# Three more places for the raw output weights of layer 0's feed-forward, and another scratch tile for layer 1's squares

## The chip, the cores and the metric

One core of one Trainium2 chip runs the whole kernel in one launch. The metric is the device time of one execution in microseconds (us); shown is the median of several runs. The engines are TensorE (PE in the profile), VectorE (DVE), ScalarE (ACT), GpSimd (POOL) and SyncE (SP), which issues nearly all transfers.

## The reference

Two layers over 512 latent tokens (x) and 256 context tokens (ctx), model width 1024. Each layer is a mixer (attention) followed by a SwiGLU feed-forward, both behind an RMS norm that is scaled, shifted and gated by a modulation worked out from the conditioning. Cut to what the change touches:

```
x   = x   + gx2 * swiglu(rms(x,   norm_ffn_w) * (1 + scx2) + shx2, ffn_w_in, ffn_w_out)   # layer 0, 512 tokens
ctx = ctx + gc2 * swiglu(rms(ctx, norm_ffn_w) * (1 + scc2) + shc2, ffn_w_in, ffn_w_out)   # layer 0, 256 tokens
swiglu(h) = (silu(gate) * up) @ w_out,   gate, up = split(h @ w_in)                       # hidden width 2816
hx  = rms(x, norm_mix_w) * (1 + scx1) + shx1                                              # start of layer 1
rms(x, w) = x * rsqrt(mean(x*x) + 1e-6) * w
```

## The kernel before

Tokens are handled in six tiles of 128: t = 0 to 3 are latent, 4 and 5 context. The hidden width 2816 is handled in 22 F-tiles of 128 (f = 0 to 21). Every fp32 operand of a matrix product is split in two: a high part (a cast on ScalarE) and a low part (raw minus high, a subtraction mostly on VectorE); each product is then three matmuls, high x high, high x low, low x high. `split_into` (lines 1023 to 1026) does this for both operands of the output product.

`way_out0` (from line 1028) is the second half of layer 0's feed-forward, hidden times `ffn_w_out`. Its 12 sums (6 token tiles x 2 halves of the width) don't fit the PSUM banks at once, so it makes two passes over the F-tiles: pass 0 (p = 0) for t = 4, 5, 0 and pass 1 for t = 1, 2, 3, six sums each. For each F-tile `ready_hid` loads the hidden tile from DRAM (tile `raw`, line 1041) and the weight tile of 128x1024 (tile `wr`, named wdr in the profile, line 1043) and splits both; then `sums` does 6 x 3 matmuls (lines 1057 to 1059). The last two F-tiles are held back (`held = 2`) and are summed bank by bank, so that the residual of one bank (`residual`, lines 480 and 481) runs under the next bank's matmuls. Four of the six banks of pass 1 are banks that pass 0 has used; pass 1 can write them when their residuals are done.

Places in SBUF:

- Raw weights come from a ring of two places, tag "raw" (`raw_tile`, line 90), which also serves other loads of the kernel. A place is free again when the low part of its tile is done.
- Split weights of pass 0 go into four fixed places (`places`, parts of the tile hT), so F-tile f waits until TensorE has finished f-4. Raw hidden tiles have two places (`raws`).
- Pass 1 splits into tiles of the pool of this stage (`out0`), with tags "wdh" and "wdl" for the weights, three places each. Pass 0 doesn't use these.

A hook in the loop advances the modulation of layer 1 (`mod_stream`), which loads 512 KB tiles (modw, line 211) in the same time and works on them on ScalarE, VectorE and GpSimd; other hooks finish norms and load early weights of layer 1.

Behind `way_out0` layer 1 begins. `factor` (line 329) squares a token tile on ScalarE with the sum as a second output and works out the norm's factor on GpSimd. The squares themselves are not wanted; they are written to a scratch tile, `spare`, for t = 1, 2 and 3. `last_norm0(t)` (line 1630) takes two tiles, h and hc: h is x times the factor (line 345, GpSimd, in `norm_steps`), which TensorE transposes (line 352); hc takes the transposes scaled and shifted (lines 358 and 360), which are then split into hT. The tiles come from the ring "xo" of six places that also holds the token tiles, but for t = 1 one of the two is `spare`. TensorE's order there is: sums of t = 4, norm of t = 1, sums of t = 5, norm of t = 2, half the sums of t = 0, norm of t = 3.

TensorE's instructions keep the order in which the program is written (a manual schedule). Those of the other engines, SyncE's transfers among them, are ordered by a planner that runs the program against modelled times: of what is ready, the earlier in the program goes first. Each engine then works through its own queue in order.

Of the kernel before, what the change touches and what calls it, by code (L numbers as in the profile page):

```python
# [11 lines left out]
F32 = mybir.dt.float32  # L12
# [7 lines left out]
P = 128  # L20
D = 1024
KT = D // P
# [41 lines left out]
def backbone(es: ExitStack, tc: tile.TileContext, x, c, ctx, c_ctx, mod_w, mod_b, norm_mix_w, norm_ffn_w,  # L64
# [25 lines left out]
    def raw_tile(shape, name):  # L90
        return keep.tile(shape, F32, name=name, tag="raw", bufs=2)
# [208 lines left out]
    def gate_row(l, part, i, pool):  # L300

        if (l, part, i) not in gmem:
            gate_mem(l, part, 1)
        g = pool.tile([P, D], F32, name=f"g{i}", tag=f"g{i}")
        with tc.issue_after(turn["load"].ins):
            nc.sync.dma_start(g.rearrange("p (k c) -> p k c", c=P), dram_rows(gmem[l, part, i]))
        return g
# [26 lines left out]
    def norm_steps(t, xt, l, f, pool, tags=(("nh", 2), ("nhc", 2)), room=None, bank=tr_tile, to=None, pool_scale=False, r=None):  # L334

        i = 0 if t < NTX else 1
        h, hc = room or (pool.tile([P, KT, P], F32, name=name, tag=tag, bufs=n)
                         for name, (tag, n) in zip(("nh", "nhc"), tags))  # L340
        halves = hc if isinstance(hc, list) else [hc[:, 0:4], hc[:, 4:8]]
        xt = xt.rearrange("p (k c) -> p k c", c=P)
        r = factor(xt, h) if r is None else r
        if pool_scale:
            turn["pool_scale"] = nc.gpsimd.tensor_scalar(h, xt, r, 1.0, ALU.mult, ALU.mult)
        else:
            turn[f"scaled{t}"] = nc.scalar.activation(h, xt, AF.Copy, scale=r)
        yield
        for g in range(2):
            pt = bank("npt", [P, 4, P])  # L350
            for k in range(4):
                turn["npt"] = nc.tensor.transpose(pt[:, k, :], h[:, 4 * g + k, :], ident)  # L352
            ks = slice(4 * g, 4 * g + 4)
            for k in range(4):
                kk = 4 * g + k
                sc, sh = aff[l][:, f, kk, i:i + 1], modc[l][:, 3 * f, kk, i:i + 1]
                if g:
                    nc.scalar.activation(halves[g][:, k], pt[:, k, :], AF.Identity, bias=sh, scale=sc)
                else:
                    nc.vector.tensor_scalar(halves[g][:, k], pt[:, k, :], sc, sh, ALU.mult, ALU.add)  # L360
            hi, lo = (to(j, g) if to else tile_T(j, t)[:, ks] for j in range(2))
            turn["hi"] = nc.scalar.copy(hi, halves[g])
            (nc.gpsimd if g and not pool_scale else nc.vector).tensor_sub(lo, halves[g], f32(hi))
# [113 lines left out]
    def residual(xt, ps, g, n, pool=None, eng=nc.vector, rb=2):  # L477

        tmp = ps if pool is None else pool.tile([P, 512], F32, name="rtmp", tag="rtmp", bufs=rb)
        nc.vector.tensor_mul(tmp, ps, g[:, n * 512:(n + 1) * 512])  # L480
        eng.tensor_add(xt[:, n * 512:(n + 1) * 512], xt[:, n * 512:(n + 1) * 512], tmp)
# [541 lines left out]
    def split_into(to, src):  # L1023
        hi, lo = to
        nc.scalar.copy(hi, src)
        nc.vector.tensor_sub(lo, src, f32(hi))

    def way_out0(xs, hidm, pool, places, raws, hook, hooks, done):

        held = 2  # L1030
        g = [gate_row(0, 5, i, pool) for i in range(2)]
        for p, tiles in enumerate(((4, 5, 0), (1, 2, 3))):
            banks = [p_1.tile([P, 512], F32, name="dps", tag=tag) for tag in (("tr0", "tr1"), ("acc0", "acc1"))[p]]
            banks += [singles.pool.tile([P, 512], F32, name="dps", tag=tag, bufs=2) for tag in ("p1", "p1", "p0", "p0")]
            sums_of = [(t, n) for t in tiles for n in range(2)]
            ready = {}

            def ready_hid(f):
                raw = pool.tile([P, 3, P], F32, name="hr", tag="hr", bufs=3) if p else raws[f % len(raws)]
                for a, b, t in ((0, 2, 4), (2, 3, 0)) if not p else ((0, 3, 1),):  # L1040
                    nc.sync.dma_start(raw[:, a:b], hidm[f][:, t * P:(t + b - a) * P].rearrange("p (t c) -> p t c", c=P))
                wr = raw_tile([P, D], "wdr")
                turn["load"] = nc.sync.dma_start(wr, ffn_w_out[0, f * P:(f + 1) * P, :])
                if p:
                    w = [pool.tile([P, 4, 256], F32R, name=name, tag=name, bufs=3) for name in ("wdh", "wdl")]
                    h = [pool.tile([P, 3, P], F32R, name=name, tag=name, bufs=3) for name in ("hdh", "hdl")]
                else:
                    w, h = places[f % len(places)]
                split_into(w, wr.rearrange("p (k c) -> p k c", k=4))
                split_into(h, raw)  # L1050
                ready[f] = h, w

            def sums(f, i):
                (t, n), ps = sums_of[i], banks[i]
                hh, hl = (z[:, tiles.index(t)] for z in ready[f][0])
                a, b = (z[:, 2 * n:2 * n + 2, :] for z in ready[f][1])
                nc.tensor.matmul(ps, hh, a, start=f == 0, stop=False)
                nc.tensor.matmul(ps, hh, b, start=False, stop=False)
                nc.tensor.matmul(ps, hl, a, start=False, stop=f == NF - 1)

            for f in range(NF - held):
                ready_hid(f)
                for i in range(len(sums_of)):
                    sums(f, i)
                hook(p, f)
                for call in hooks.get((p, f), ()):
                    call()
            for f in range(NF - held, NF):
                ready_hid(f)
            for i, (t, n) in enumerate(sums_of):  # L1070
                for f in range(NF - held, NF):
                    sums(f, i)
                residual(xs[t], banks[i], g[0 if t < NTX else 1], n)
                done(t, n)
# [115 lines left out]
    for t in CTX_FIRST:  # L1190
        h = start.pool.tile([P, D], F32, name="nh", tag="nh", bufs=2)
# [125 lines left out]
    if True:  # L1317
# [93 lines left out]
        i = len(steps) - 1  # L1411
# [216 lines left out]
            late.pop(0)[1]()  # L1628

    def last_norm0(t):  # L1630
        h, hc = (spare if t == 1 and not i else raw_tile([P, KT, P], "nhc") if t == 2 and i else
                 keep.tile([P, KT, P], F32, name="nh", tag="xo", bufs=6) for i in range(2))
        with tc.high_priority(300):
            for _ in norm_steps(t, xs[t], 1, 0, None, room=(h, hc), pool_scale=True, r=factors.get(t)):
                pass

    if True:
# [8 lines left out]
        spare = keep.tile([P, KT, P], F32, name="nh", tag="xo", bufs=6)  # L1646
# [6 lines left out]
        for t in CTX_FIRST[:2]:  # L1653
            first.sums(t, banks[t], range(KT))
            ready(t)
            last_norm0(t - 3)
        first.sums(0, banks[0], range(4))
        last_norm0(3)
        first.sums(0, banks[0], range(4, KT))
        ready(0)  # L1660
# [311 lines left out]
```

## Time and profile before

| | us |
|---|---|
| median of 3 runs (lowest to highest) | 1685.1 (1684.14 to 1687.23) |
| profiled execution | 1686.72 |
| its span | 1684.9 |
| TensorE busy in it | 1629.0 (97%) |
| VectorE busy | 1145.2 (68%) |
| ScalarE busy | 934.8 (55%) |
| GpSimd busy | 713.2 (42%) |

The granted TensorE clock was 0.994 of full speed over the span. Rows of a timeline read: start, duration, engine, line, operation, output <- input, shape, count, and in brackets how long the engine had been idle before and what ended the idle time. Rows of windows read: stretch, its length, then busy time and count of TensorE, its weight loads, VectorE, ScalarE and GpSimd, then granted clock, busy share of the 16 DMA engines, GB/s. Rows of waits read: engine and line, what it waited for, total us, times, longest. All times in rows are us from the span's start.

### The profile page before, as it was taken

Reading aid. Unit: us, or ns where it says so; the run is one execution under the profiler, and the core shown is the slowest. Engines: PE = TensorE matmul, PEld = TensorE weight load, DVE = VectorE, ACT = ScalarE, POOL = GpSimd, SP = SyncE. Lnnn points to the kernel's source line nnn. Section 1 sums busy time; section 2 is a strip of 40 time slices with the busy share of each in tenths; the row PEclk is TensorE's granted clock in tenths of the full one; section 3 lists DMA queues with packets and bytes.
Section 4 is the critical chain, followed back from the end, with each engine's and each line's share of the span. In section 5 each row is a group of like instructions: output and inputs, shape, how many; then the busy total and the mean of one; then the engine's idle time right before and its main releaser. Section 6 shows DMA issues by size and latency. Waiting matters only on the chain. (4 is left out here: it accounts for less than half of the span.)

```text
span 1684.9 us, 28521 instructions
## 1 busy us (share of the span) xinstructions
PE 1629.0 (97%) x10376; PEld 1467.9 (87%) x10376; DVE 1145.2 (68%) x1980; ACT 934.8 (55%) x2008; POOL 713.2 (42%) x872
## 2 busy tenths in 40 slices
PE   6999999899999999999999999999999999999998
PEld 3977787677999999998878799999988899999887
DVE  3765756554799987767767666666666598887433
ACT  5466665745455655544564456666666555555320
POOL 2665555621345554412413367766765332221000
PEclk8999999999999999999999999999999999999999
DMA  9221321421455555439965221111113333331431
GB/s 321 70 71 52 93 70 51 163 63 38 120 178 173 166 159 164 135 110 334 305 185 192 91 58 44 48 42 47 45 51 100 113 96 110 104 105 53 138 100 63
DMA packets 221692, 194.67 MB, mean 116 GB/s; under 512 B 20016, under 2 KB 206960, under 8 KB 221552
## 3 DMA queue, kind: packets, MB, share of 16 engines
q1 hardware_dynamic: 221200, 192.65, 36.9%
q8 instruction: 81, 1.33, 0.3%
q14 instruction: 59, 0.48, 0.1%
q10 hardware_dynamic: 352, 0.21, 0.0%
HBM read 179.94 MB, written 12.87 MB: 114 GB/s over the span
## 5 line engine op out<-in xcount | busy, mean ns | idle before, releaser
L928 ACT CAST wbh<-wr 128x512 fp32r<-128x512 f32 x170 | 104.8, 621 | 122.9 <-PE p L960 67.7
L960 PE MATMUL p<-hT,wbh 128*128 128x256 f32 (+1 forms) x752 | 154.1, 298 | 0.0
L474 PE MATMUL inps<-wih,hT 128*128 128x384 f32 x512 | 143.9, 343 | 2.4 <-ACT qkv L688 1.7
L938 POOL TENSOR_TENSOR wbl<-wr,wbh 128x512 fp32r<-128x512 f32 x43 | 58.9, 1369 | 174.2 <-ACT wbh L928 174.2
L960 PEld LDWEIGHTS p<-hT,wbh 128*128 128x128 f32 x752 | 122.1, 191 | 0.2
L938 DVE TENSOR_TENSOR wbl<-wr,wbh 128x512 fp32r<-128x512 f32 x127 | 107.8, 860 | 19.8 <-ACT wbh L928 15.8
L960 PE MATMUL p<-hT,wbl 128*128 128x256 f32 (+1 forms) x376 | 111.8, 297 | 0.0
L960 PE MATMUL p<-t,wbh 128*128 128x384 f32 (+1 forms) x480 | 110.9, 317 | 0.0
L231 POOL TENSOR_TENSOR modp<-modp 128x512 f32<-128x512 f32 x40 | 57.5, 1437 | 111.8 <-ACT modp L230 111.8
L613 POOL TENSOR_SCALAR Pt<-Pt,rc 128x256 f32<-128x256 f32 (+3 forms) x96 | 75.3, 796 | 66.1 <-DVE rc L610 58.5
L960 PE MATMUL p<-hTt,wbh 128*128 128x256 f32 (+1 forms) x480 | 100.9, 302 | 0.0
L914 POOL TENSOR_TENSOR wr<-wr 128x512 f32<-128x512 f32 x40 | 62.2, 1556 | 91.1 <-DVE ws L919 88.8
L474 PEld LDWEIGHTS inps<-wih,hT 128*128 128x128 f32 x512 | 93.4, 188 | 5.4 <-ACT qkv L688 2.8
L960 PE MATMUL p<-b,wbh 128*128 128x384 f32 x368 | 93.5, 335 | 0.6 <-DVE c L988 0.6
L928 ACT CAST wbh<-ws 128x512 fp32r<-128x512 f32 x120 | 69.5, 580 | 43.7 <-PE p L960 28.5
L224 DVE SCALAR_TENSOR_TENSOR ma<-modw,cols,ma 128x256 f32<-128x256 f32 x140 | 91.5, 654 | 2.3
L601 ACT ACTIVATE Pt<-sc,nm 128x256 f32<-128x256 f32 (+3 forms) x96 | 67.7, 708 | 34.0 <-DVE nm L597 16.0
L474 PE MATMUL inps<-wil,hT 128*128 128x384 f32 x256 | 85.8, 335 | 0.0
L938 DVE TENSOR_TENSOR wbl<-ws,wbh 128x512 fp32r<-128x512 f32 x120 | 81.7, 681 | 1.7 <-ACT wbh L928 1.6
L960 PEld LDWEIGHTS p<-t,wbh 128*128 128x128 f32 x480 | 82.8, 189 | 0.0
L960 PEld LDWEIGHTS p<-hTt,wbh 128*128 128x128 f32 x480 | 78.4, 191 | 3.0 <-ACT modp L230 2.1
L474 PE MATMUL inps<-wihi,hT 128*128 128x384 f32 x256 | 76.6, 356 | 2.1 <-DVE modc L279 1.9
(357 smaller groups left out, 5219.1 us busy)
## 6 DMA issues: line engine op xcount, KB each, us to landing
modw<-in_mod_w_dram SPq DMA_DIRECT2D x96, 512.0 KB, 4.8
wr<-in_ffn_w_in_dram SPq DMA_DIRECT2D x176, 256.0 KB, 3.0
wdr<-in_ffn_w_out_dram SPq DMA_DIRECT2D x66, 512.0 KB, 3.6
wir<-in_od_w_in_dram SPq DMA_DIRECT2D x96, 128.0 KB, 2.3
hidm<-hid SPq DMA_DIRECT2D x44, 192.0 KB, 1.9
hr<-hidm SPq DMA_DIRECT2D x22, 192.0 KB, 3.5
x<-in_x_dram SPq DMA_DIRECT2D x8, 512.0 KB, 3.6
wir<-in_ev_w_in_dram SPq DMA_DIRECT2D x16, 256.0 KB, 3.4
```

Source lines behind the costliest of these rows:

```text
L224: nc.vector.scalar_tensor_tensor(acc, w[:, k], scale[k], acc, ALU.mult, ALU.add)
L231: nc.gpsimd.tensor_add(pr[:, 0:2], pr[:, 0:2], pr[:, 2:4])
L474: nc.tensor.matmul(ps, hs[j][:, k, :], ws[k // 2][z][:, k % 2, c0:c1], start=(k, j, z) == (0, 0, 0), stop=(k, j, z) == (KT - 1, 1, 0))
L601: turn["exp"] = nc.scalar.activation(p[:, :n], s, AF.Exp, bias=nm[:, c1], accum_out=sm[:, c1])
L613: nc.gpsimd.tensor_scalar(p[:, :n], p[:, :n], rc[:, hh:hh + 1], 1.0, ALU.mult, ALU.mult)
L914: nc.gpsimd.tensor_sub(w, raw[f, "G1"], w)
L928: nc.scalar.copy(hi, w)
L938: (nc.gpsimd if name == "G2" else nc.vector).tensor_sub(lo, raw[need[n]], f32(hi))
L960: nc.tensor.matmul(ps, w[:, k, :], H[b][h][:, k, :], start=first and k == 0 and q == 0, stop=final and k == 3 and q == 2, skip_group_check ...
```

## The change

In `ready_hid`, pass 0 takes the raw weight tile of f = 0 to 8 from the ring "raw" as before; from f = 9 on it takes it from the pool of the stage, with the tag "wdl" and three places, the ring in which pass 1 later puts its low parts (same size). Pass 1's raw weights come from the ring "raw" as before. In `last_norm0`, `spare` for t = 1 is now hc and no longer h; h is a tile of the ring "xo". The squares still write `spare`, which is thus a different tile from h.

```
                 for a, b, t in ((0, 2, 4), (2, 3, 0)) if not p else ((0, 3, 1),):
                     nc.sync.dma_start(raw[:, a:b], hidm[f][:, t * P:(t + b - a) * P].rearrange("p (t c) -> p t c", c=P))
-                wr = raw_tile([P, D], "wdr")
+                wr = (raw_tile([P, D], "wdr") if p or f < 9 else
+                      pool.tile([P, D], F32, name="wdr", tag="wdl", bufs=3))
                 turn["load"] = nc.sync.dma_start(wr, ffn_w_out[0, f * P:(f + 1) * P, :])
...
     def last_norm0(t):
-        h, hc = (spare if t == 1 and not i else raw_tile([P, KT, P], "nhc") if t == 2 and i else
+        h, hc = (spare if t == 1 and i else raw_tile([P, KT, P], "nhc") if t == 2 and i else
                  keep.tile([P, KT, P], F32, name="nh", tag="xo", bufs=6) for i in range(2))
```

More of the change, by code (lines that the diff above doesn't have):

```diff
@@ L1041, in ready_hid @@
                     nc.sync.dma_start(raw[:, a:b], hidm[f][:, t * P:(t + b - a) * P].rearrange("p (t c) -> p t c", c=P))
-                wr = raw_tile([P, D], "wdr")
+                wr = (raw_tile([P, D], "wdr") if p or f < 9 else
+                      pool.tile([P, D], F32, name="wdr", tag="wdl", bufs=3))
                 turn["load"] = nc.sync.dma_start(wr, ffn_w_out[0, f * P:(f + 1) * P, :])
@@ L1630, in last_norm0 @@
     def last_norm0(t):
-        h, hc = (spare if t == 1 and not i else raw_tile([P, KT, P], "nhc") if t == 2 and i else
+        h, hc = (spare if t == 1 and i else raw_tile([P, KT, P], "nhc") if t == 2 and i else
                  keep.tile([P, KT, P], F32, name="nh", tag="xo", bufs=6) for i in range(2))
```

## The prediction, as recorded before the result was known

> **What bounds the kernel now.** I read the page first, then busy time by stretch around the changed code, then what TensorE waited for there, and last the rows of each engine in time.
>
> ```profile
> PE 1629.0 (97%) x10376; PEld 1467.9 (87%) x10376; DVE 1145.2 (68%) x1980; ACT 934.8 (55%) x2008; POOL 713.2 (42%) x872
> ```
>
> ```profile
> 840.00:850.00 10.00, 7.60 (x33) 5.74 (x32) 6.50 (x8) 6.03 (x10) 3.12 (x2) 1.00 0.73 228
> 850.00:860.00 10.00, 8.64 (x36) 6.20 (x35) 7.75 (x11) 6.04 (x9) 1.48 (x4) 1.00 0.66 213
> ```
>
> ```profile
> PE dps L1057 <- DVE x L481: 1.4, 3, 0.9
> PE npt L352 <- POOL nh L345: 1.3, 1, 1.3
> PE dps L1057 <- ACT hT L1025: 1.3, 1, 1.3
> PE dps L1058 <- DVE hT L1026: 1.1, 1, 1.1
> PE inps L474 <- DVE hT L363: 0.6, 1, 0.6
> ```
>
> TensorE is busy for 97% of the span of 1684.9 us, so only its gaps can be won: 56 us in all. In the two passes of way_out0 (about 759 to 951 us) it has gaps in one place, around 840 to 860 us, where pass 0 ends and pass 1 begins: 2.40 + 1.36 us by the second fence. The third fence (TensorE's waits from 720 to 1000 us) names the causes: two waits on the split of pass 0's last weights (L1025 on ScalarE, L1026 on VectorE), three on residual additions of pass 0 (L481), and, after way_out0, one on the scaling of layer 1's norm (L345 on GpSimd). The first two causes belong to the first edit, the last to the second.
>
> What a gap costs is more than the wait, since the matmuls after it also come slower. So I count matmuls. The rows are TensorE's, in time.
>
> ```profile
> 833.84 0.39 PE L1057 MATMUL dps<-hT,hTt 128*128 128x512 f32 x1
> ...
> 842.00 0.39 PE L1057 MATMUL dps<-hT,hTt 128*128 128x512 f32 x1
> ...
> 853.13 0.39 PE L1057 MATMUL dps<-wdh,hdh 128*128 128x512 f32 x1
> ...
> 858.75 0.40 PE L1057 MATMUL dps<-wdh,hdh 128*128 128x512 f32 x1
> ```
>
> From 833.84 to 842.00 stand 36 undisturbed matmuls: 8.16 us, 0.2267 each, so an F-tile of 18 takes 4.08. The 36 of the last two F-tiles, 842.00 to 853.13, take 11.13: 2.97 lost. The first 15 of pass 1, 853.13 to 858.75, take 5.62 instead of 3.40: 2.22 lost. Together 5.19 us.
>
> **First edit: places for raw weights.** The rows are SyncE's, ScalarE's and VectorE's.
>
> ```profile
> 833.25 0.46 SPq L1043 DMA_DIRECT2D wdr<-in_ffn_w_out_dram  x1
> ...
> 835.75 6.37 SPq L1043 DMA_DIRECT2D wdr<-in_ffn_w_out_dram  x2
> ```
>
> ```profile
> 839.45 1.05 ACT L1025 CAST hT<-wdr 128x1024 fp32r<-128x1024 f32 x1 [4.01 <-DMA wdr<-in_ffn_w_out_dram]
> ...
> 843.10 1.03 ACT L1025 CAST hT<-wdr 128x1024 fp32r<-128x1024 f32 x1
> ```
>
> ```profile
> 834.49 1.23 DVE L1026 TENSOR_TENSOR hT<-wdr,hT 128x1024 fp32r<-128x1024 f32 x1 [1.19 <-ACT hT L1025]
> ```
>
> ```profile
> SPq L1043 <- DVE hT L1026: 22.7, 18, 2.4
> ```
>
> The raw ring has two places, and 18 of the weight loads wait for the low split that frees one (last fence, SyncE's waits from 745 to 862 us). The row at 834.49 splits f=19 and ends at 835.72; f=21's load is issued at 835.75 into that place. f=20's, issued at 833.25, can be cast only at 839.45. So a place is held for about 6.2 us of transfer and 2.3 of cast and low split, 8.5 in all; two places give one tile per 4.25 us, while TensorE takes one per 4.08. The reserve wears off, and f=21's cast at 843.10 comes after TensorE's f=20 products for the first bank.
>
> From f=9 on the change gives three places of its own. Three of 8.5 us give a tile per 2.8 us, so the transfer no longer sets the pace; the four places of split weights do, which keep a tile ready up to four ahead (16.3 us). f=21 can then be split when TensorE is done with f=17, about 12 us before it is needed. The first loss, 2.97, goes. ScalarE and VectorE do the same casts and low splits as before, only earlier; no instruction is added, and the DMA count and bytes stay.
>
> The second loss is one step further on. The rows are ScalarE's and VectorE's.
>
> ```profile
> 852.00 1.05 ACT L1025 CAST wdh<-wdr 128x1024 fp32r<-128x1024 f32 x1 [1.53 <-DMA wdr<-in_ffn_w_out_dram]
> ```
>
> ```profile
> 851.64 0.69 DVE L480 TENSOR_TENSOR dps<-dps,g 128x512 f32<-128x512 f32 x1
> 853.08 1.23 DVE L1026 TENSOR_TENSOR wdl<-wdr,wdh 128x1024 fp32r<-128x1024 f32 x1 [0.74 <-ACT wdh L1025]
> 854.22 0.69 DVE L480 TENSOR_TENSOR dps<-dps,g 128x512 f32<-128x512 f32 x1
> 854.82 0.68 DVE L481 TENSOR_TENSOR x<-x,dps 128x512 f32<-128x512 f32 x1
> ```
>
> Between the multiply (851.64) and the add (854.82) that free a bank, VectorE stands idle for pass 1's third weight tile, cast at 852.00 when its transfer lands. In the changed kernel the two raw places are free from the splits of f=7 and f=8 on (about 790 us), so pass 1's first two tiles load some 50 us earlier. Their low halves need places of the ring that now holds pass 0's raw weights; these come free with the splits of f=19 to f=21, before the residuals. Residual pairs then run behind TensorE: the third bank's products end three pairs of F-tile sums (3 x 1.36 = 4.1 us) before pass 0's end, pass 1 wants that bank 1.36 us after it, and a pair of multiply and add takes 1.3 us. Even three low splits of 1.23 between them fit the 5.4 us. I take the whole 2.22.
>
> What could eat it: f=9, 10 and 11 need no earlier tile, so SyncE can issue them early, when the first loads of pass 0 are still under way.
>
> ```profile
> 780.00:800.00 20.00, 20.00 (x90) 16.58 (x89) 14.97 (x21) 11.07 (x20) 9.00 (x8) 1.00 1.02 345
> ```
>
> ```profile
> 768.00:770.00 2.00, 2.00 (x11) 1.65 (x10) 1.82 (x4) 0.73 (x1) 0.00 (x0) 1.00 1.10 348
> ...
> 825.00:830.00 5.00, 5.00 (x24) 4.14 (x23) 4.86 (x7) 3.83 (x8) 1.98 (x2) 1.00 0.87 273
> 830.00:835.00 5.00, 5.00 (x24) 4.14 (x23) 3.81 (x6) 3.22 (x7) 2.66 (x4) 1.00 0.74 221
> ```
>
> ```profile
> 763.19 0.51 ACT L1025 CAST hTt<-hTt 128x384 fp32r<-128x384 f32 x1 [4.99 <-PE dps L1058]
> ...
> 784.28 1.06 ACT L1025 CAST hT<-wdr 128x1024 fp32r<-128x1024 f32 x1 [0.79 <-DMA wdr<-in_ffn_w_out_dram]
> ```
>
> ```profile
> L1057 PE MATMUL dps<-hT,hTt x132: 387/389/502, 759.0 to 852.5; 128*128 128x512 f32 x132
> ```
>
> At 768 us the DMA engines move 348 GB/s at a share over 1, so three loads of 512 KB ahead of the others cost these at most 4.5 us. f=8 is cast at 784.28 and split by 788; TensorE starts at 759.0 and wants f=8 after 8 x 4.08 us, at 791.6. A delay of 4.5 would miss that by 0.9 us; I take 0, since some of that delay falls into time in which the splits wait for TensorE anyway (763.19, f=4, 4.99 us), and keep 0 to 4.5 us for the range. It cannot go below nothing: TensorE is busy for all of 780 to 800, so nothing is to be won there.
>
> [...]
>
> **Second edit: the square's scratch.** The rows are TensorE's and GpSimd's, then the readers of x.
>
> ```profile
> 953.89 0.28 PE L474 MATMUL inps<-wil,hTc 128*128 128x256 f32 x1
> 954.01 0.28 PE L474 MATMUL inps<-wih,hTc 128*128 128x256 f32 x1
> 955.64 1.09 PE L352 MATMUL npt<-cst,nh 128*128 128x128 f32 x8 [1.34 <-POOL nh L345]
> ```
>
> ```profile
> 948.88 0.55 POOL L160 TENSOR_TENSOR rs_n<-rs_n,neghalf 128x1 f32<-128x1 f32 x1
> ...
> 954.47 1.12 POOL L345 TENSOR_SCALAR nh<-x,rs_n 128x1024 f32<-128x1024 f32 x1 [2.25 <-ACT nh L331]
> ...
> 957.10 1.12 POOL L345 TENSOR_SCALAR nh<-x,rs_n 128x1024 f32<-128x1024 f32 x1
> ```
>
> ```profile
> L347 ACT ACTIVATE nh<-x,rs_n x3: 1151/1152/1160, 855.0 to 876.0; 128x1024 f32<-128x1024 f32 x3
> ```
>
> The squares of t=1, 2 and 3 all write the tile spare, and before the change h of t=1 is that tile. Its factor is ready at 949.43 (948.88 + 0.55), yet the scaling starts at 954.47, after the last square. After the change h of t=1 is another tile of the ring and only hc, written after the transposes, is spare. The tiles of x that way_out0 is done with (t=4, 5, 0) were read last by 877.2, so three places are free: spare, h of t=1, h of t=2. The scaling can run at about 949.5 and end by 950.7, and the transposes follow the sums at once. The gap from 954.01 to 955.64 less the usual 0.12 is 1.51 us. Next on that path is h of t=2, used after 3.2 us of sums and 0.8 of transposes, 958.1 in the old count; it ended at 958.22 with GpSimd late and comes some 5 us sooner now. hc's wait for the last square is over before its first write. Bounds: 0 to 1.51; I take 1.51, and 0.5 us back for TensorE meeting the later wait on L363 (0.6 us in the third fence) sooner.
>
> **Sum.** 2.97 + 2.22 + 1.51 - 0.5 = 6.2 us. The profiled execution took 1686.72, 1.6 above the median of 1685.1; it would take 1680.5, and the median 1678.9, say 1679.
>
> **Rivals.** First, transfers are the bound: then places only change the order of waiting, the first edit gives nothing and the second 1.5: 1683.6. For it speaks the share over 1 until 825 us, against it the unfilled 825 to 835. Second, the early loads delay f=6 to f=8, TensorE wants these before the reserve has grown, and the whole bound of 4.5 us opens as a gap before f=9: 1683.4. Third, slower: pass 1's first two low halves are ready when their raw tiles land (about 800 us), and if they take two of the three places then, f=12 to f=21 go through one, held for 8.5 us. That is 4.4 us a tile over TensorE's pace: ten tiles cost 44 us, less the 16.3 of reserve, 28 in place of the 2.97; with the other gains about 1706. It decides from the sixth or seventh such tile on. Against it: pass 0's loads stand first in program order and have been waiting for a place all along. Fourth, the second edit only swaps its wait for one on another engine: 1680.4. Fifth, the queues of all engines but TensorE are ordered anew behind the change, and layer 1's attention gives back what was won:
>
> ```profile
> 1240.00:1260.00 20.00, 17.68 (x109) 15.98 (x108) 13.35 (x27) 12.58 (x32) 13.42 (x24) 0.92 0.16 53
> 1260.00:1280.00 20.00, 17.36 (x117) 14.74 (x115) 13.75 (x24) 14.58 (x34) 9.83 (x16) 0.99 0.49 159
> ```
>
> Its gaps here are 2.32 + 2.64 = 5.0 us; if they double, 1684.
>
> **How the numbers follow.** Forecast 0.52, fourth rival 0.13, first 0.15, second 0.08, third 0.05, fifth 0.07. A measurement here tells 0.2% (3.4 us) from no change, so faster means under 1681.7: 0.52 + 0.13 = 0.65. Slower, above 1688.5, are the third and 0.02 of the fifth, should its gaps more than double: 0.07. The rest, 0.28, is the same. The range goes from 1676 (6.2 plus some 3 us of kinder order) to 1685 (past the first, second and fifth rivals). Forecast alone: 1677 to 1681.
>
> **What would show it.** TensorE's first 15 matmuls of pass 1 in 3.4 us and the 36 before them in 8.2; no wait of L1057 or L1058 on ScalarE or VectorE; loads at L1043 for f=9 on that wait less; pass 1's first casts before the end of pass 0; the first L345 about 4 us before the transposes. Wrong would be a gap between 780 and 800 us, loads of f=12 on each waiting for TensorE's next tile, or new waits after 1000 us.

## The result and the profile after

The changed kernel takes 1688.86 us (median of 21 runs, 1686.83 to 1696.15), the kernel before 1685.05 in the same session: ratio 1.0027, 95% interval 1.0019 to 1.0035. It is 3.8 us slower; 1679 was forecast. The profiled execution took 1687.98, its span 1686.2. From L1043 on the lines of the changed kernel stand one higher (weight load L1044, sums L1058 to L1060).

Both forecast gains are in the trace, and more is lost in a place that was clean before. First the groups of the sums, with the first and last start in each; then TensorE's first matmul behind the two passes.

```profile
L1058 PE MATMUL dps<-hT,hTt x132: 387/389/629, 757.0 to 857.4; 128*128 128x512 f32 x132
L1058 PE MATMUL dps<-wdh,hdh x132: 387/389/500, 858.0 to 953.9; 128*128 128x512 f32 x132
```

```profile
954.55 0.27 PE L293 MATMUL gps<-cst,modc 128*8 128x128 f32 x1
```

Pass 0 (its first matmul to pass 1's first) takes 101.0 us, pass 1 (to L293) 96.5. Before, by the same rows (759.0, 853.13, 951.16), they took 94.1 and 98.0. So pass 1 gained 1.5, pass 0 lost 6.9, and together the passes lost 5.4. If the second edit gives its forecast 1.5 back behind them, 3.9 are left, near the 3.8 between the medians. That this fits so well is in part chance, since it compares one execution of each kernel: that of before lies 1.7 above its median, that of the changed kernel 0.9 below. The latter also starts the passes 2.0 us earlier, ahead of the first load that is changed (764.75 below), so the two spans differ by 1.3 only.

Busy time by stretch after the change, columns as before:

```profile
780.00:800.00 20.00, 18.44 (x82) 14.95 (x81) 13.84 (x17) 13.47 (x23) 6.28 (x6) 1.00 1.06 364
800.00:820.00 20.00, 19.41 (x93) 15.19 (x92) 16.13 (x22) 11.58 (x20) 7.99 (x8) 1.00 0.95 311
820.00:840.00 20.00, 18.89 (x81) 14.69 (x80) 17.54 (x22) 12.94 (x24) 7.71 (x7) 1.00 0.87 274
840.00:850.00 10.00, 6.68 (x23) 5.01 (x22) 5.90 (x6) 1.60 (x4) 4.14 (x3) 0.83 0.78 252
850.00:860.00 10.00, 10.00 (x46) 8.28 (x45) 8.01 (x12) 6.30 (x11) 4.60 (x6) 1.00 0.19 53
```

What TensorE waited for, 720 to 1000 us:

```profile
PE dps L1060 <- DVE hTt L1026: 4.9, 4, 3.3
PE dps L1059 <- DVE hT L1026: 1.6, 1, 1.6
...
PE dps L1059 <- DVE wdl L1026: 0.6, 1, 0.6
PE inps L474 <- DVE hT L363: 0.3, 1, 0.3
```

The old waits on pass 0's last weights, on the residuals (L481) and on L345 are gone, and 850 to 860 us, where pass 1 starts, is full. In their place stand one wait of 1.6 us on the low half of a weight tile and four, 4.9 together, on the low half of the *hidden* tile, an operand that the prediction's steps hardly name.

The first new wait, near 791 us, is f=8's. SyncE's queue and VectorE's:

```profile
764.75 2.32 SPq L1044 DMA_DIRECT2D wdr<-in_ffn_w_out_dram  x4
...
774.02 0.33 SPq L1044 DMA_DIRECT2D wdr<-in_ffn_w_out_dram  x1
...
778.65 0.38 SPq L1044 DMA_DIRECT2D wdr<-in_ffn_w_out_dram  x1
```

```profile
785.84 1.76 DVE L1026 TENSOR_TENSOR hT<-wdr,hT 128x1024 fp32r<-128x1024 f32 x1
...
788.78 1.21 DVE L1026 TENSOR_TENSOR hT<-wdr,hT 128x1024 fp32r<-128x1024 f32 x1
...
790.31 1.21 DVE L1026 TENSOR_TENSOR hT<-wdr,hT 128x1024 fp32r<-128x1024 f32 x1
```

Four loads go out together at 764.75 (f=6 and, free to go, f=9 to f=11); f=7 follows at 774.02 and f=8 at 778.65. The tiles that came early are also split early, so f=8's low half is third in the row and ends at 791.52; TensorE starts on it at 791.58.

The largest one is the gap before the third matmul of f=19. TensorE, then VectorE, ScalarE and SyncE:

```profile
840.78 0.39 PE L1059 MATMUL dps<-hT,hTt 128*128 128x512 f32 x1
844.49 0.61 PE L1060 MATMUL dps<-hT,hTt 128*128 128x512 f32 x1 [3.32 <-DVE hTt L1026]
...
848.24 0.39 PE L1060 MATMUL dps<-hT,hTt 128*128 128x512 f32 x1
```

```profile
836.19 0.55 DVE L1026 TENSOR_TENSOR hTt<-hTt 128x384 fp32r<-128x384 f32 x1
836.66 3.44 DVE L224 SCALAR_TENSOR_TENSOR ma<-modw,cols,ma 128x256 f32<-128x256 f32 x4
840.01 1.22 DVE L1026 TENSOR_TENSOR hT<-wdr,hT 128x1024 fp32r<-128x1024 f32 x1
841.33 2.11 DVE L1026 TENSOR_TENSOR wdl<-wdr,wdh 128x1024 fp32r<-128x1024 f32 x1
843.36 1.07 DVE L1026 TENSOR_TENSOR hTt<-hTt,hTt 128x384 fp32r<-128x384 f32 x1
```

```profile
838.19 0.50 ACT L1025 CAST hTt<-hTt 128x384 fp32r<-128x384 f32 x1
```

```profile
831.87 0.80 SPq L1041 DMA_DIRECT2D hTt<-hidm  x2
...
836.77 0.81 SPq L1041 DMA_DIRECT2D hTt<-hidm  x2
...
844.46 0.81 SPq L1041 DMA_DIRECT2D hTt<-hidm  x2
```

f=19's hidden tile is cast by 838.69, and its low half starts only at 843.36. In between VectorE works through its queue: four products of the modulation, the low half of a weight tile that is wanted later, and that of a weight tile of pass 1 (wdl). f=20's hidden load goes out at 836.77, when f=18's low half is done (836.19 + 0.55), and f=21's at 844.46, right behind f=19's: the raw hidden tiles have only two places. The nine matmuls from 844.49 to 848.24 then take 3.75 us in place of 2.04 at the 0.2267 each of before: the granted clock is down to 0.50 there.

### The profile page after: what moved, and what is told of

Read it like the earlier page. It is cut to its first block, busy times and chain, and to the rows that moved or that the text cites. A ratio compares the mean times of both kernels' runs of the same rounds, so it can differ in the third digit from the quotient of the medians.

```text
span 1686.2 us, 28490 instructions
## 1 busy us (share of the span) xinstructions
PE 1627.6 (97%) x10376; PEld 1465.6 (87%) x10376; DVE 1143.4 (68%) x1980; ACT 934.2 (55%) x2008; POOL 706.6 (42%) x872
## 5 line engine op out<-in xcount | busy, mean ns | idle before, releaser
L960 PE MATMUL p<-hTt,wbh 128*128 128x256 f32 (+1 forms) x480 | 100.9, 302 | 0.0
```

The lines of the kernel that those rows point to most:

```text
L960: nc.tensor.matmul(ps, w[:, k, :], H[b][h][:, k, :], start=first and k == 0 and q == 0, stop=final and k == 3 and q == 2, skip_group_check ...
```

## The experiments

My theory: the loss is the first edit's; it has two parts, the early loads (gap at f=8) and the hidden tile's late low half (gap at f=19), and the latter comes from the two raw hidden places or from VectorE's order. Rivals: the second edit costs; transfers are the bound; the modulation crowds pass 0 out. "Difference" is that of the medians against the kernel before in the same session (its medians there are 1685.05 for the changed kernel, 1684.86 for e_edit1, e_edit2, e_hid3 and e_pri, 1684.08 for e_hidonly, e_ord, e_ord_hid3 and e_p1late, 1684.65 for the last three). The ratio is an estimate from all runs and need not be that of the medians. Pass times are read as above, good to about 0.1 us, and come from one profiled execution each, which can lie far from the median: that of e_hid3, 1686.76, is the slowest of 12, that of e_hidonly, 1681.02, the fastest of 12.

| kernel | median | difference | ratio, 95% interval | pass 0 | pass 1 |
|---|---|---|---|---|---|
| before | 1685.1 | | | 94.1 | 98.0 |
| changed | 1688.86 | +3.8 | 1.0027, 1.0019 to 1.0035 | 101.0 | 96.5 |
| e_edit2 | 1683.13 | -1.7 | 0.9985, 0.9975 to 0.9995 | 96.2 | 96.8 |
| e_edit1 | 1689.38 | +4.5 | 1.0031, 1.0020 to 1.0042 | 100.6 | 96.3 |
| e_hid3 | 1681.73 | -3.1 | 0.9981, 0.9970 to 0.9991 | 96.0 | 96.9 |
| e_pri | 1688.42 | +3.6 | 1.0024, 1.0014 to 1.0034 | 100.9 | 96.4 |
| e_hidonly | 1684.28 | +0.2 | 1.0007, 0.9996 to 1.0018 | 91.1 | 100.5 |
| e_ord | 1682.50 | -1.6 | 0.9990, 0.9981 to 0.9998 | 94.3 | 97.2 |
| e_ord_hid3 | 1678.60 | -5.5 | 0.9967, 0.9955 to 0.9979 | 91.1 | 96.6 |
| e_p1late | 1683.38 | -0.7 | 0.9998, 0.9990 to 1.0007 | 94.7 | 97.5 |
| e_mod | 1688.12 | +3.5 | 1.0015, 1.0006 to 1.0024 | 92.5 | 104.6 |
| e_ord_p1late | 1683.03 | -1.6 | 0.9989, 0.9980 to 0.9998 | 92.9 | 97.3 |
| e_both | 1678.33 | -6.3 | 0.9959, 0.9947 to 0.9972 | 91.2 | 96.6 |

**e_edit2, e_edit1: each edit alone.** The kernel before with the edit of `last_norm0`, and the changed kernel without it.

> The kernel before with the second edit alone (the square's scratch); the raw weights of the output product keep their two places. Theory (the loss lies in the first edit: the low half of pass 0's hidden tiles comes late, and a 3.3 us gap of TensorE lowers its clock; the second edit by itself does what was forecast): 1.0 to 1.6 us faster than the kernel before, ratio about 0.9991; TensorE has no wait on L345 and is busy for all of 940 to 960 us; the end of pass 0 keeps its waits on L1025 and L1026 of about 2.4 us. Rival A (the second edit shifts the queues of ScalarE, VectorE and GpSimd, and the loss is in layer 1): 2 us or more slower than the kernel before. Rival B (the two edits only together): no change.

> The changed kernel without its second edit: three more places for raw weights from f=9 on, the square's scratch as before. Theory (the loss is in the first edit): slower than the kernel before by 5 to 6 us (the 3.8 measured for both edits plus the 1.5 of the second), about 1690 to 1691; in the profile waits of TensorE on the low half of the hidden tile near 820 to 845 us, the longest about 3.3 us, and on the weight low of f=8 near 791 us, about 1.6. Rival A (the second edit costs): about as fast as the kernel before or up to 2 us faster. Rival B (only together): no change.

The second edit alone gains 1.7 us, near the 1.51 forecast, though the interval of the ratio allows 0.8 to 4.2. The first alone loses 4.5, a little less than the 5 to 6 expected, with the changed kernel's waits. Rivals A and B fall. In e_edit2 the late weights of f=20 and f=21 stay, as they must. TensorE's rows:

```profile
844.90 0.50 PE L1057 MATMUL dps<-hT,hTt 128*128 128x512 f32 x1 [1.16 <-ACT hT L1025]
846.45 0.77 PE L1058 MATMUL dps<-hT,hTt 128*128 128x512 f32 x1 [1.05 <-DVE hT L1026]
847.02 0.63 PE L1059 MATMUL dps<-hT,hTt 128*128 128x512 f32 x1
...
849.98 0.39 PE L1057 MATMUL dps<-hT,hTt 128*128 128x512 f32 x1
```

These are the same two waits as in the kernel before, whose rows are:

```profile
844.18 0.50 PE L1057 MATMUL dps<-hT,hTt 128*128 128x512 f32 x1 [1.34 <-ACT hT L1025]
845.74 0.50 PE L1058 MATMUL dps<-hT,hTt 128*128 128x512 f32 x1 [1.06 <-DVE hT L1026]
...
847.69 0.39 PE L1057 MATMUL dps<-hT,hTt 128*128 128x512 f32 x1
```

From the second gap's end eight matmuls take 1.95 us before and 3.53 in e_edit2. A near-identical pair of gaps thus cost 1.6 us more in one execution than in the other, by the clock: 0.63 was granted over 846 to 848 us and 0.52 over 848 to 850 in e_edit2, 1.00 over both in the kernel before. That is most of the 2.1 us by which pass 0 of e_edit2's profile is longer, though its median is lower.

**e_hid3: three raw places for the hidden tiles of pass 0.**

```
-  raw = pool.tile([P, 3, P], F32, name="hr", tag="hr", bufs=3) if p else raws[f % len(raws)]
+  raw = pool.tile([P, 3, P], F32, name="hr", tag="hr", bufs=3) if p or f >= 9 else raws[f % len(raws)]
```

> The changed kernel, with the raw hidden tiles of pass 0 from f=9 on in three places of their own (the ring that pass 1 uses for them) in place of the two fixed ones. Theory, first half (the two raw places of the hidden tiles hold up their loads, since f's load waits for the low half of f-2, and that low half now stands behind other work): the waits of TensorE on the hidden tile's low half (4.9 us in the changed kernel) shrink to under 1.5 us, and with them the stretch at half clock; 3 to 5 us faster than the changed kernel, about 1684 to 1686. Theory, second half (it is VectorE's order, not the places): the hidden tiles land earlier, but their low halves still come behind the weights' lows and the products of the modulation; under 1 us of change. Rival (transfers are the bound, so more tiles in flight land no sooner): no change, the loads' medians from issue to landing rise by what the waits before them fall. In all cases the wait near 791 us on f=8's weights stays, since the early loads are still there.

3.1 us faster than before, 6.9 better than the changed kernel by the two differences: more than expected. The waits on the hidden tile are gone. As expected the wait on f=8 stayed, and in this execution it was 3.0 us, with a stretch of lower clock of its own (0.57 granted over 796 to 798 us), in TensorE's rows:

```profile
795.91 0.50 PE L1059 MATMUL dps<-hT,hTt 128*128 128x512 f32 x1 [2.98 <-DVE hT L1026]
...
796.62 0.63 PE L1058 MATMUL dps<-hT,hTt 128*128 128x512 f32 x1
...
799.89 0.39 PE L1060 MATMUL dps<-hT,hTt 128*128 128x512 f32 x1
```

**e_pri: the hidden split ahead in the planner.**

```
-                split_into(h, raw)
+                with tc.high_priority(0 if p else 300):
+                    split_into(h, raw)
```

> The changed kernel, with the split of pass 0's hidden tiles put ahead in the order of ScalarE and VectorE; places as changed. Theory, second half (VectorE's order: low halves of weights that are not wanted for some 12 us, of pass 1 too, and products of the modulation stand ahead of the low half of the hidden tile): the waits on the hidden tile's low half fall from 4.9 to under 1.5 us, and the kernel is 3 to 5 us faster than the changed one. Theory, first half (the places): the last hidden tile is still issued near 844 us, so the wait of 3.3 us stays, and the change is under 1 us. Rival (transfers): no change.

No gain; the hidden tile's waits are 5.1 us (longest 2.4). But the edit did not do what it says where it matters: VectorE's queue at the end of pass 0 still has the modulation's products, the weights' low halves and pass 1's ahead of the same hidden tile. It says nothing on the order; e_p1late asks that again.

**e_hidonly: hidden places without weight places.** The kernel before, with the second edit and the line of e_hid3.

> The kernel before with the second edit and with three places of their own for pass 0's raw hidden tiles from f=9 on; the raw weights keep their two places (the first edit is left out). Theory (with the weights' places freed the hidden tiles became the limit; in the kernel before the weights were it, as the prediction said): the late weights of f=20 and f=21 stay, with 2 to 3 us of gap around 840 to 850 us, no gap near 791; about as fast as the second edit alone (1683 on the last chip, 0.9985 of before), the hidden places worth under 1 us. Rival (the hidden places are all the gain, the weights' places nothing): as fast as the changed kernel with three hidden places or faster, 0.9981 or less, and no wait on the weights' split at the end of pass 0.

Neither faster nor slower than before (+0.2). The expectation was wrong about the place: in the profiled execution pass 0 is clean (91.1 us) although the weights have two places, and the whole loss stands at pass 1's start. VectorE, then TensorE:

```profile
846.64 0.69 DVE L480 TENSOR_TENSOR dps<-dps,g 128x512 f32<-128x512 f32 x1
848.54 1.23 DVE L1026 TENSOR_TENSOR wdl<-wdr,wdh 128x1024 fp32r<-128x1024 f32 x1 [1.21 <-ACT wdh L1025]
849.69 0.68 DVE L481 TENSOR_TENSOR x<-x,dps 128x512 f32<-128x512 f32 x1
```

```profile
852.21 0.80 PE L1057 MATMUL dps<-wdh,hdh 128*128 128x512 f32 x1 [3.13 <-DVE x L481]
```

This is the prediction's second loss in a larger size: VectorE stands between a multiply and its add for a late weight tile of pass 1. This execution took 1681.0, the fastest of its kernel's runs, so it does not show where the median's other 3 us are lost; that stays open. It does show that two weight places can keep TensorE's pace in pass 0: from the end of f=8's low half to that of f=21's a tile takes 4.09 us here (786.17 to 839.35) and took 4.44 before (787.98 to 845.69). The prediction's 4.25 came from how long a single tile held its place.

**e_ord: loads in the order of the F-tiles.**

```
+                with behind(*("load",) * (not p and f >= 9)):
                     turn["load"] = nc.sync.dma_start(wr, ffn_w_out[0, f * P:(f + 1) * P, :])
```

> The changed kernel, with SyncE's loads of pass 0's raw weights from f=9 on kept in the order of the F-tiles, each issued behind the load of the F-tile before it, so that f=9 to f=11 no longer go ahead of f=7 and f=8. Theory (two separate losses: the early loads cost the gap of 1.6 to 3 us near 791 us, the hidden tiles' two places the 3.3 us at the end): the first gap goes, the second stays; 1 to 3 us faster than the changed kernel, 1685 to 1687, still no faster than the kernel before plus its second edit. Rival (the early loads started it all: the hidden tiles are late at the end only because pass 0 was set back at its start): both gaps go, about 6 us faster than the changed kernel, 1681 to 1683.

The wait at f=8 goes, so the early loads were its cause. The second gap did not stay as the theory had it: it shrank to waits of 0.8 at most, as TensorE's waits show. The gain, 5.4 us on the changed kernel, is nearer to the rival's 6 than to the theory's 1 to 3. How the order of the loads acts on the second gap is not shown.

```profile
PE dps L1061 <- DVE hTt L1026: 1.9, 4, 0.8
PE dps L1060 <- DVE wdl L1026: 1.3, 1, 1.3
```

**e_p1late: pass 1's first three weight splits behind pass 0's last.** The casts and low halves of pass 1's f=0 to 2 are queued behind the last hidden cast and low half of pass 0:

```
+                with behind(*("cast0", "low0") * (p and f < 3)):
                     split_into(w, wr.rearrange("p (k c) -> p k c", k=4))
```

> The changed kernel, with the splits of pass 1's first three weight tiles queued behind the last splits of pass 0 on ScalarE and VectorE. The reordering of pass 0's hidden splits left VectorE's queue at the end of pass 0 as it was, so this asks again what the order is worth. Theory (the places decide): f=21's hidden load is still issued only when f=19's low half is done, near 840 us; at most two low halves of pass 1 (1.2 and 2.1 us) come out of the way, so the last wait of 3.3 us shrinks to about 1 to 2 us, and what is gained there (1 to 2 us, with the clock perhaps 1.8 more) comes back in part at the start of pass 1: 0 to 3 us faster than the changed kernel. Rival (VectorE's order decides): no wait on the hidden tile above 0.6 us, 4 us or more faster than the changed kernel.

Here the rival held: 4.5 us better than the changed kernel, and no wait on the hidden tile over 0.6. VectorE's order decides much of the last gap. TensorE's wait on the hidden tile:

```profile
PE dps L1063 <- DVE hTt L1026: 0.8, 2, 0.6
```

So the 3.3 us gap needs its causes together: hidden tiles that land late for want of places, weights' low halves ahead of theirs, and a pass 0 set back by the early loads. Take one away and it falls under 1 us; its 1.7 us of half clock go with it (1.00 is granted over 840 to 850 us in e_hid3, e_ord and e_p1late, 0.83 in the changed kernel).

**e_ord_hid3: loads in order and three hidden places.**

> Both remedies: the changed kernel with loads in the order of the F-tiles and three places for pass 0's raw hidden tiles from f=9 on. Theory: neither gap, pass 0 takes its 22 x 4.08 = 89.8 us within 1 us; 3 to 4 us faster than with the three hidden places alone (its 3.0 us wait at f=8 and the stretch at lower clock behind it), 6 to 8 us faster than the kernel before, ratio 0.9955 to 0.997, about the 1679 of the prediction. Rival (transfers are the bound: with loads in order the tiles come late by what was won): no faster than 0.998 of before, with waits on a load's cast between 800 and 850 us.

The theory holds in the main: no gap in pass 0, 1678.60, ratio 0.9967. The sizes fall short: 5.5 us faster than before in place of 6 to 8, and 2.4 faster than e_hid3 by the two differences in place of 3 to 4. Pass 0 takes 91.1 in place of 89.8; 12 matmuls of the modulation stand in it, which the 22 x 4.08 leave out. Busy time by stretch:

```profile
780.00:800.00 20.00, 20.00 (x90) 16.54 (x89) 17.02 (x22) 14.94 (x26) 7.53 (x8) 1.00 1.06 378
800.00:820.00 20.00, 20.00 (x96) 16.02 (x95) 16.50 (x24) 11.21 (x21) 6.10 (x6) 1.00 1.02 351
820.00:840.00 20.00, 20.00 (x90) 16.57 (x89) 18.66 (x23) 13.03 (x25) 10.87 (x8) 1.00 0.93 310
840.00:850.00 10.00, 10.00 (x45) 8.27 (x45) 9.58 (x14) 3.67 (x8) 5.79 (x6) 1.00 0.73 243
```

TensorE is full from 780 to 850 us at a DMA share of up to 1.06: the transfers carry the pace. Against e_hidonly, which lacks only the weights' places (with two places no load can go early, so there is no order to mend), it is 5.7 us faster by the two differences. Against e_edit2, which lacks the hidden places as well, it is 3.8 us faster by the differences. So the first edit is worth some 4 to 6 us once the hidden tiles and the order of loads don't take it away; the open 3 us of e_hidonly are in the larger figure.

**e_mod: the modulation out of pass 0's second half.** In the loop, `if f % 10 < 9 if p == 0 else f > 7` became `if f < 9 if p == 0 else f > 0`.

> The changed kernel, with the hook that advances the modulation of layer 1 called in pass 0 only for f=0 to 8 and in pass 1 for f=1 on (before: nearly all of pass 0, and f=8 on in pass 1); the same work, later. That takes the 512 KB loads and VectorE's products from the second half of pass 0. Rival (transfers are the bound in pass 0): the waits on the hidden tile's low half near 818 to 848 us go, and the DMA share of 800 to 840 us falls below 0.7; 4 us or more faster than the changed kernel unless pass 1 or the work behind it gives that back. Theory (places and the order of queues): f=21's hidden load still waits for f=19's low half; VectorE's products no longer stand ahead of that low half (3.4 us of them at 836 us), so the last wait shrinks to 0 to 2 us; 1 to 4 us faster there, while the early gap near 791 us stays, and layer 1's modulation comes late by as much as was moved, so that the total lies within 2 us of the changed kernel or is slower.

Pass 0 falls to 92.5 us, but pass 1 takes 104.6, and the total hardly moves (+3.5 against +3.8). In part that is TensorE's own work for the modulation, 12 matmuls that moved from pass 0 to pass 1. The gap at f=19 goes, but this run takes the transfers and VectorE's products out of pass 0 together, so it doesn't tell these apart. e_ord_hid3, with the modulation in place and no gap, shows that the transfers need not cost anything (TensorE full from 780 to 850 us at a DMA share of up to 1.06).

**e_ord_p1late and e_both: order with late splits of pass 1, and all three.**

> The changed kernel with loads in the order of the F-tiles and with pass 1's first three weight splits behind the last splits of pass 0; pass 0's raw hidden tiles keep their two places. Theory A (the places of the hidden tiles are a cause of their own): waits on the hidden tile's low half of about 1.9 us stay, as with the order alone, and the start of pass 1 has waits on residuals (L481) of 0.5 us or more; 1681 to 1683, slower than with three hidden places by 2 to 4 us. Theory B (the order of the queues is the whole cause): as fast as the version with order and three hidden places, 0.9967 of before within 0.1%.

> All three remedies in one: loads in the order of the F-tiles, three places for pass 0's raw hidden tiles from f=9 on, pass 1's first three weight splits behind the last splits of pass 0. Theory A (order and places leave no gap of pass 0 for the third remedy to close): no faster than with two remedies, 0.9967 of before within 0.1%; if anything up to 1 us slower, since low halves of pass 1 now stand between the residuals at its start. Theory B (each remedy adds its own share): another 1 to 2 us faster, 0.996 or less.

Theory A of the first held in its time: without the hidden places the gain stays at 1.6 us, as with the order alone. The waits that it named did not come: those on the hidden tile are 0.9 in total, and there is none on L481. Where the rest of the 3.9 us to e_ord_hid3 is lost stays open. e_both is at 0.9959 and e_ord_hid3 at 0.9967. Theory A (within 0.1%) and Theory B (0.996 or less) of e_both both allow that; the intervals overlap and the pass times agree within 0.1 us, so a gain of the third remedy is not shown. Both beat the kernel before and the changed one.

## Why the prediction was wrong

*Start of pass 1: right.* Forecast 3.4 us for the first 15 matmuls; they take from 858.03 to 861.43, 3.40, by TensorE's rows of the changed kernel:

```profile
849.86 0.40 PE L1058 MATMUL dps<-hT,hTt 128*128 128x512 f32 x1
...
858.03 0.39 PE L1058 MATMUL dps<-wdh,hdh 128*128 128x512 f32 x1
...
861.43 0.39 PE L1058 MATMUL dps<-wdh,hdh 128*128 128x512 f32 x1
```

Pass 1 as a whole gained 1.5, not 2.22: the new wait of 0.6 us on a low half of its own (wdl, in the waits above) is in it.

*End of pass 0: right for the tiles it looked at.* The 36 matmuls of f=20 and f=21 take 8.17 us (849.86 to 858.03 in the same fence; forecast 8.2). The loss moved to f=19 and before. The reason given was too simple: a tile per 4.25 us from two places, against 4.08, loses 2.2 us over the 13 tiles behind f=8, less than the 3.7 by which f=8's low half was ready ahead of its matmuls (787.98, 791.73). And e_hidonly has a pass 0 as clean as that of e_ord_hid3 with the two places kept.

*Second edit: right.* 1.51 forecast (1.0 with the 0.5 given back), 1.7 measured alone; GpSimd scales t=1 at once behind its factor (its rows in the changed kernel; 5.0 us lay between them before):

```profile
952.27 0.55 POOL L160 TENSOR_TENSOR rs_n<-rs_n,neghalf 128x1 f32<-128x1 f32 x1
952.92 1.14 POOL L345 TENSOR_SCALAR nh<-x,rs_n 128x1024 f32<-128x1024 f32 x1
```

The 0.5 us given back for L363 was not needed: that wait is 0.6 in e_edit2 as before, and 0.3 in the changed kernel.

*The step that failed* is the sentence that ScalarE and VectorE do the same casts and low splits "only earlier", with no instruction added and so no cost. On an engine that works through one queue, earlier means ahead of something. The steps said who waits for the weights' low halves and never asked what would now stand behind them. It was the hidden tile's: same split, same engines, two raw places, and needed for every F-tile. TensorE waited 4.9 us on it in the changed kernel, with 1.7 of half clock behind the longest wait, and had no such wait before. e_p1late and e_hid3 each recover it from one side. I had named the sign of it as one of the things that would show me wrong (a gap between 780 and 800 us), but only for the loads.

*The term that was mis-sized* is "What could eat it": I took 0 of a bound of 4.5 us for f=8. The wait was 1.6 in the changed kernel and 3.0 in e_hid3. The bound held for the wait alone; with the half clock behind it pass 0 of e_hid3 is 4.9 longer than that of e_ord_hid3 (96.0 and 91.1), past the 4.5. The reason for 0 (the splits wait for TensorE anyway) did not hold, since VectorE takes the early tiles' low halves first (785.84, 788.78) and f=8's third.

*The rivals.* Transfers as the bound: refuted by e_ord_hid3, where TensorE is full at 780 to 800 us at 378 GB/s and at 800 to 820 us at 351. What I had counted for this rival, a share over 1 until 825 us, was misread: by windows of 5 us the kernel before has 0.97 at 800 and 0.80 at 805. This rival's 0 of 5.19 us for the first edit did not come true either: it is worth some 4 to 6 us by the differences above. Early loads: the mechanism was right, its price part of the loss. Pass 1's low halves: I had them take places; what they took was time on VectorE, just ahead of a tile that was due. The second edit swapping its wait: no. Layer 1's attention: its two stretches are at 17.70 and 17.02 us of 20 busy, 17.68 and 17.36 before; no doubling.

With both remedies the sum comes near the forecast: pass 0 94.1 - 2.97 = 91.1 (measured 91.1), pass 1 98.0 - 2.22 = 95.8 (96.6), in all 6.2 us (5.5). That the total of 1678.60 is so close to 1679 owes something to the session, in which the kernel before took 1684.08 and not 1685.05. And the remedies are not in the prediction: the changed kernel as it was forecast lost.

## What to carry to other kernels

When places are added for one operand of a product, ask for the other operand what its places are, and where its steps stand in each queue; the resource that was freed lets work run ahead, and what runs ahead in an engine's queue pushes something back (here the hidden tile's low half, with 4.9 us of TensorE's waits). Count not only who waits for the work that comes earlier but what is due in the queue just behind it. Where several tiles can be loaded early, issue them in the order in which they are used (e_ord: 5.4 us on the changed kernel).

## What the hardware showed that I had not expected

In the changed kernel the clock made a gap of TensorE half as long again. Behind the wait of 3.32 us the granted clock was 0.50 for 3.41 us (clock third from the end):

```profile
844.74:848.15 3.41, 3.41 (x9) 2.62 (x9) 0.70 (x1) 0.00 (x0) 0.28 (x1) 0.50 0.79 249
```

That is 1.7 us beside the 3.3 of the wait. Behind the wait of 2.98 us in e_hid3 it was 0.57 over 796 to 798 us, and behind that of 3.13 in e_hidonly 0.83 over 850 to 860 us, as 3.4 us at 0.50 would give. In e_edit2 it was 0.63 over 846 to 848 us and 0.52 over 848 to 850, behind two waits of 1.16 and 1.05 us, one matmul apart, while behind 1.34 and 1.06 in the kernel before it stayed at 1.00.

From 42 to 1300 us the granted clock of the changed kernel changes at 42.60, 844.74, 848.15, 1257.75 and 1261.16 us, which are 235, 1, 120 and 1 steps of 3.413 us apart. From 48 to 1300 us that of the kernel before changes at 48.53, 1256.85 and 1260.26 us, 354 and 1 such steps apart. What sets these times is not shown. The first row is e_edit2's, for the 3.41 us ahead of its lower clock; the others are the kernel before's, for two stretches of that length around its two gaps:

```profile
843.11:846.52 3.41, 1.19 (x5) 0.44 (x3) 1.54 (x2) 1.99 (x5) 1.26 (x1) 1.00 0.66 199
```

```profile
840.42:843.84 3.42, 2.42 (x11) 1.68 (x9) 1.69 (x2) 2.85 (x7) 0.51 (x1) 1.00 0.60 185
843.84:847.25 3.41, 2.01 (x8) 1.43 (x9) 2.13 (x2) 1.50 (x3) 0.76 (x1) 1.00 0.81 229
```

TensorE was busy for 1.19 of 3.41 us in the first, and a lower clock followed. It was busy for 2.42 and 2.01 in the others, and the clock stayed. In other stages of the kernel before, stretches with 1.7 us idle had either behind them: 1.00 behind 195.30 to 198.71 us and 0.50 behind 1253.44 to 1256.85. What decides it is not shown. So the length of a gap alone did not tell its price here, and single executions differ by it: the eight matmuls behind the second gap took 1.95 us in the kernel before and 3.53 in e_edit2.
